# The down projection of 18 f tiles by Strassen's recursion, in three rounds

## The chip, the core and the metric

The kernel runs on one NeuronCore of a Trainium2 chip. The metric is the device time of one execution in microseconds (us); lower is better. The engines are TensorE (PE, matmuls), VectorE (DVE), ScalarE (ACT), GpSimd (POOL, hardly used here) and SyncE (SP, which issues the transfers).

## The reference

One layer of a diffusion backbone on 128 context and 512 latent tokens, 640 in all, with 1024 channels: modulation from a condition vector, an mLSTM and a convolution branch with an output projection, and then the gated MLP, to which the change belongs:

```python
h2 = rmsnorm(x, p['norm2_g']) * (1 + sc2) + sh2
gate, val = jnp.split(jnp.einsum('btd,df->btf', h2, p['w_up']), 2, axis=-1)
gate = dwconv_grid(gate, p['ffn_dw_w'], p['ffn_dw_b'])      # 3x3; on context width 3
x = x + g2 * jnp.einsum('btf,fd->btd', jax.nn.gelu(gate) * val, p['w_down'])
...
return final rmsnorm(x)
```

All is float32. `w_down` is 2816 x 1024: 22 tiles of 128 rows (the f tiles) by 8 tiles of 128 output channels (m). `g2` is one of six vectors that a 1024 x 6144 matrix makes from the condition.

## The kernel before

Activations lie channels first: a tile holds 128 channels and the 640 tokens, in two halves of 320 (`HALF`). A float32 product is made of three faster ones: each operand is split into a high part, rounded to the type fp32r, and a low part, the rest (hi and lo), and `three` adds hi x hi, hi x lo and lo x hi in one PSUM accumulator. ACT makes the high part by a copy, DVE the low part by a subtraction. Weights come in groups of eight 128 x 128 blocks (`BLOCKS`, in the order of use; `load` fetches a group to one of `NST` = 3 buffers `wst`, `prep` makes `wh` and `wl`, `NWT` = 3 of each).

The program's order is fixed when it is built: each engine runs its own list of instructions strictly in that order and waits by semaphores. `_Order` sets it: it follows the emission of the matmuls with an estimate of time and puts in between what the other engines have to do. A side task is a generator (`spawn`), which `step` carries on after every third of a product; `later` puts small pieces of DVE work into lanes, which are filled in where DVE has room, and `need(tag)` emits all that is left of a tag at once. In lane 20 stand the products of the condition with the rest of its matrix (`ada_tile`, in the trace `junk<-ad`, 128 of them, DVE alone); the last 32 carry the tag `g2`, the gate of the MLP's residual.

The MLP goes by f tiles. `ffn_tile(f)` emits the 48 matmuls of the gate half and the 48 of the value half (8 channel tiles, three products, two halves). ACT copies the gate to a grid buffer (`gbuf`), nine taps of the convolution run on DVE (`ffn_tap`, into `acc`), ACT applies gelu (`ge`), DVE multiplies with the value in PSUM, and ACT and DVE split the result (`ah`, `al`; the last tiles in another pool as `acth`, `actl`). Two lists set the stages: `UPS` (f 0 to 11, then 12 to 21) and `DNS` (f 0 to 10 after the first, f 11 to 21 after the second up stage). The first down stage makes each of the eight output tiles from 11 f tiles with 66 matmuls of 128 x 128 x 320, and `residual` adds it to `x2[m]` with three DVE operations (`x<-mm,mods,x`: context and latent tokens have different gates, so the first half is two pieces). Ahead of it `need("g2")` stands in the up stage, before tile 8. The second down stage runs by token parts, first 384 tokens (`dnA`; three output tiles begin without the last f tile), then 256 (`dnB`), each followed by the final norm (`final`) and the output's transfers.

PSUM has three pairs of accumulators (`mm`) and two single ones (`ps`).

Of the kernel before, what the change touches and what calls it, by code (L numbers as in the profile page):

```python
# [9 lines left out]
F32 = mybir.dt.float32  # L10
F32R = mybir.dt.float32r
# [4 lines left out]
P = 128  # L16
# [41 lines left out]
HOLE = 600.0  # L60
NB = 15
# [9 lines left out]
NST = 3  # L71
# [10 lines left out]
def _blocks():  # L82

    b = []
    held = {0: 2, 1: 3}
    for k in range(KD):
        b += [(nm, k, m) for nm, m in FIRST]
    for nm, m in ORDER:
        if nm == "v":
            held[len(b) // GB] = len(b) // GB + NWT  # L90
            held[len(b) // GB + 1] = 0
            b += [("v", k, 2 * m + i) for k in range(KD) for i in range(2)]
        else:
# [30 lines left out]

class _Timed:
# [192 lines left out]
def tile_trunk(  # L318
# [79 lines left out]
    ready = {}  # L398
    lines = {}

    def load(g):
        if g in stage or g in ready or g >= NGRP:
            return
        t = od.ring("st", sp.tile([P, GB * P], F32, tag="st", name="wst"), NST)
        Q.dma_start(t, w_d[g])
        stage[g] = t

    def prep(g):

# [12 lines left out]

        ready[g] = (hi, lo)
        lines[g] = od.spawn(parts())

    state = {"g": -1}

    def W(b, width=P):
        g, o = divmod(bidx[b], GB)
        if g > state["g"]:  # L430
            state["g"] = g
            held = HELD.get(g)
            for gg in range(g, g + NWT if held is None else held):
                prep(gg)
            if g >= NSTART:
                for gg in range(g + NWT, g + NWT + NST - 1):
                    load(gg)
# [716 lines left out]
    def A2(shape, dt=F32, name="b"):  # L1154
        return ap2.tile(shape, dt, tag="B", name=name)
# [181 lines left out]
    def ffn_gate(f, pgt):  # L1337
        od.need(("ffn", f - 2))
        g = gb_[f % 2]
        S.activation(g[:, 0:NCTX], pgt[:, 0, 0:NCTX], AF.Copy)  # L1340
        S.activation(lat_rows(g)[:, 0:3, 0:GRID_W], pgt[:, 0, NCTX:TH].rearrange("p (r w) -> p r w", w=GRID_W), AF.Copy)
        S.activation(lat_rows(g)[:, 3:8, 0:GRID_W], pgt[:, 1, 0:TH].rearrange("p (r w) -> p r w", w=GRID_W), AF.Copy)
        accs[f] = acc = A([P, TF], name="acc")
        for i in range(9):
            od.later(("ffn", f), lambda i=i: ffn_tap(f, g, acc, i), f % 2)

    def ffn_out(f, pvt):
        while od.waits(("ffn", f)):
# [9 lines left out]
        if f in range(0, NACT2) or f in range(NFH + 1, NFH + 1 + NACT2):  # L1358
            hi, lo = A2([P, T], F32R, "ah"), A2([P, T], F32R, "al")
        else:  # L1360
            hi, lo = A([P, T], F32R, "acth"), A([P, T], F32R, "actl")
        yield
        S.activation(hi, ge, AF.Copy)
        yield
        V.tensor_sub(lo, ge, hi.bitcast(F32))
        acts[f] = (hi, lo)

    def ffn_act(f, pvt):
        t_act[f] = od.spawn(ffn_out(f, pvt))
# [32 lines left out]
        mhalf(mat, 1, range(KD), h2, rng, pt=pts[2][:, h, 0:TH])  # L1402
    ffn_gate(1, pts[2])
    ffn_act(1, mtile("up", NF + 1, range(KD), h2))
    for f in UPS[0][2:]:
        if f == NACT2 - 2:
            od.need("g2")
        ffn_tile(f)
    ks = DNS[0]
    od.finish(t_act[UPS[0][-1]])  # L1410
    for m in range(8):
        pt = dn(mtile, "dn", m, ks)
        for h in range(2):
            residual(x2[m], pt[:, h, 0:TH], g2c[:, m, :], HALF[h])
    for f in ks:
        acts.pop(f)
    for f in UPS[1]:
        ffn_tile(f)


    ks = DNS[1]

    PARTS = [slice(0, TL), slice(TL, T)]

    def final(h, sums, adds):
# [13 lines left out]
        for j in range(0, KD, 2):  # L1439
# [19 lines left out]
    od.finish(t_f)  # L1459
    pools["stack"].close()  # L1460
# [1 line left out]
def _columns(v):  # L1462
# [129 lines left out]
```

## Time and profile before

| | |
|---|---|
| median of 3 runs | 976.29 us (974.4 to 976.96) |
| profiled execution | 975.71 us, span 973.5 us |
| PE | busy 946.8 us (97%), 6700 matmuls |
| DVE | busy 735.1 us (76%), 1348 instructions |
| ACT | busy 362.2 us (37%), 658 instructions |
| mean granted PE clock | 0.993 of full speed |

PE's busy time counts overlapping matmuls, so what one costs is read from the distance between starts. Lines are L139 for every instruction of the engines, since the wrapper `_Timed` issues them all; groups are told apart by the names of their tiles. From 540 us on the trace shows the MLP: up tiles to 665 us, the first down stage to 745 us, up tiles to 888 us, `dnA` to 930 us, `dnB` to 962 us, the last norm and output to 973.5 us.

### The profile page before, as it was taken

The numbers are of one execution on the slowest core, as the hardware profiler recorded it, in microseconds if no ns is written. First come the engines' busy times: TensorE is split into PE (matmuls) and PEld (weight loads), VectorE is DVE, ScalarE is ACT, GpSimd is POOL, SyncE is SP. The second block draws the span as 40 slices with busy tenths as digits, with TensorE's granted clock in tenths as the row PEclk, the third lists the DMA queues.
The fourth block names the chain that finished last, engine by engine and source line by source line (L and its number), as shares of the span: only waits on it lengthen the run. The fifth ranks groups of instructions, "written<-read, shape, count | busy, mean of one in ns | idle before, by whom it ended". The sixth has DMA issues, their size and how long they took to land.

```text
span 973.5 us, 16460 instructions
## 1 busy us (share of the span) xinstructions
PE 946.8 (97%) x6700; PEld 924.2 (95%) x6700; DVE 735.1 (76%) x1348; ACT 362.2 (37%) x658; POOL 6.0 (1%) x41
## 2 busy tenths in 40 slices
PE   5999999999999999999999999899999999999996
PEld 2899999999998999999989999899999999999995
DVE  3849989998897988898879778985323777675565
ACT  5553434245634422224674323232111232323342
POOL 0100000000000000000000000000000000000000
PEclk9999999999999999999999999999999999999998
DMA  9635122211242365567443221522222222123353
GB/s 355 245 104 87 45 76 66 74 47 45 87 141 71 104 196 189 201 233 251 147 135 102 77 79 63 163 87 65 82 71 65 88 68 84 65 88 94 123 170 113
DMA packets 38971, 113.01 MB, mean 116 GB/s; under 512 B 4336, under 2 KB 7280, under 8 KB 38896
## 3 DMA queue, kind: packets, MB, share of 16 engines
q1 hardware_dynamic: 38896, 111.96, 35.7%
q8 instruction: 53, 0.87, 0.4%
q14 instruction: 22, 0.18, 0.1%
HBM read 108.79 MB, written 3.15 MB: 115 GB/s over the span
## 4 chain that ended last, share of the span: by engine, by line
PE 92%; DVE 4%; ACT 2%; issue 1%; DMA 1%; SPq 0%; DVEq 0%; ACTq 0%
PE mm L139 84%; PE ps L139 8%; DVE junk L139 1%; DVE acc L139 1%; DMA x<-in_xT 1%; DVE wl L139 0%; ACT wh L139 0%; ACT h L139 0%; ACT L139 0%; DVE rsy L139 0%; DVE yo L139 0%; ACT h2h L139 0%; DVE rst L139 0%; ACT sq L139 0%; SPq L139 0%
## 5 line engine op out<-in xcount | busy, mean ns | idle before, releaser
L139 ACT ACTIVATE wh<-wst 128x1024 fp32r<-128x1024 f32 x145 | 152.9, 1057 | 197.1 <-PE mm L139 166.8
L139 DVE TENSOR_TENSOR wl<-wst,wh 128x1024 fp32r<-128x1024 f32 x145 | 176.5, 1220 | 56.2 <-ACT wh L139 55.9
L139 PE MATMUL mm<-h2h,wl 128*128 128x320 f32 x704 | 164.9, 310 | 2.4 <-DVE wl L139 2.4
L139 PE MATMUL mm<-h2h,wh 128*128 128x320 f32 x704 | 165.0, 310 | 0.6 <-ACT h2h L139 0.6
L139 PE MATMUL mm<-h2l,wh 128*128 128x320 f32 x704 | 164.8, 310 | 0.4 <-DVE h2l L139 0.4
L139 PE MATMUL mm<-hh,wh 128*128 128x320 f32 (+2 forms) x576 | 134.3, 312 | 3.5 <-ACT wh L139 2.5
L139 PE MATMUL mm<-hl,wh 128*128 128x320 f32 (+2 forms) x576 | 133.7, 311 | 0.0
L139 PE MATMUL mm<-hh,wl 128*128 128x320 f32 (+2 forms) x576 | 133.4, 310 | 0.0
L139 DVE SCALAR_TENSOR_TENSOR acc<-gbuf,cols,acc 128x455 f32<-128x455 f32 (+2 forms) x176 | 129.7, 742 | 4.4
L139 PEld LDWEIGHTS mm<-h2h,wl 128*128 128x128 f32 x704 | 119.2, 189 | 2.8 <-DVE wl L139 2.7
L139 PEld LDWEIGHTS mm<-h2h,wh 128*128 128x128 f32 x704 | 119.3, 189 | 1.3 <-ACT h2h L139 1.2
L139 PEld LDWEIGHTS mm<-h2l,wh 128*128 128x128 f32 x704 | 119.1, 188 | 1.1 <-DVE h2l L139 1.0
L139 DVE SCALAR_TENSOR_TENSOR z<-glu,cols,z 128x641 f32<-128x641 f32 (+14 forms) x120 | 102.2, 889 | 0.8
L139 PEld LDWEIGHTS mm<-hh,wh 128*128 128x128 f32 x576 | 96.0, 188 | 5.8 <-ACT wh L139 3.0
L139 PEld LDWEIGHTS mm<-hl,wh 128*128 128x128 f32 x576 | 96.6, 188 | 2.2 <-issue 1.3
L139 PEld LDWEIGHTS mm<-hh,wl 128*128 128x128 f32 x576 | 96.9, 189 | 0.7 <-issue 0.7
L139 PE MATMUL mm<-ah,wl 128*128 128x320 f32 (+2 forms) x320 | 85.6, 308 | 0.0
L139 PE MATMUL mm<-ah,wh 128*128 128x320 f32 (+2 forms) x320 | 85.4, 307 | 0.0
L139 PE MATMUL mm<-al,wh 128*128 128x320 f32 (+2 forms) x320 | 85.4, 307 | 0.0
L139 DVE SCALAR_TENSOR_TENSOR junk<-ad,cb 128x512 bf16<-128x512 f32 x128 | 81.8, 686 | 0.1
L139 PEld LDWEIGHTS mm<-ah,wl 128*128 128x128 f32 x320 | 56.8, 188 | 0.1
L139 PEld LDWEIGHTS mm<-al,wh 128*128 128x128 f32 x320 | 56.8, 188 | 0.0
(224 smaller groups left out, 1284.2 us busy)
## 6 DMA issues: line engine op xcount, KB each, us to landing
wst<-in_w SPq DMA_DIRECT2D x145, 512.0 KB, 3.6
ad<-in_ada SPq DMA_DIRECT2D x64, 256.0 KB, 3.0
adst<-in_ada SPq DMA_DIRECT2D x16, 512.0 KB, 10.2
x<-in_xT SPq DMA_DIRECT2D x16, 320.0 KB, 5.7
out_yT<-x SPq DMA_DIRECT2D x8, 192.0 KB, 4.3
cb<-in_crow SPq DMA_DIRECT2D x4, 256.0 KB, 5.0
out_yT<-yo SPq DMA_DIRECT2D x4, 256.0 KB, 2.5
Ca<-in_cst SPq DMA_DIRECT2D x1, 516.0 KB, 6.8
```

The source lines that it names most:

```text
L139: return fn(*args, **kw)
```

## The change

For f 0 to 17 the down projection is done in three rounds of six f tiles (`ROUNDS`), each after the up tiles it needs and one more (`UPS` has four lists now). A round takes three pairs of f tiles and, one after another, four groups: q = 0 to 3 is the pair of output tiles m1 = 2q and m2 = 2q + 1. With an f pair, an output pair and the two token halves, the product is one of 2 x 2 blocks, and Strassen's recursion (in Winograd's form) needs seven block products for eight. A block product here is nine matmuls of 320 columns (three f pairs, three parts), a group 63 matmuls instead of 72. The f tiles 18 to 21 stay with `dnA` and `dnB` (`LASTF`).

The seven weight forms of a group (`FORMS`; three 128 x 128 blocks side by side, 384 columns) are made on the core from two loaded groups: four sums on DVE (`sf`), and for each form a high part on ACT and a low part on DVE, both now in one buffer, a `wh` or a `wl` in turn (`prep_form`); `ahead` keeps six forms prepared. Of each f pair the activations get seven forms of 320 columns (`x_form`: four differences `tf` and `tg`, seven high and seven low parts `xf`). The intermediate sums stay in PSUM: three accumulators, `pa` with four of the products one after another, `pb` with two, `pd` with one, and `residual` reads an accumulator after each product, ten DVE operations a group. `need("g2")` moves to the start of round 0. The centre tap of the convolution goes from DVE to ACT, and at the end `final` of both parts is waited for.

```diff
-UPS = [list(range(0, NFH + 1)), list(range(NFH + 1, NF))]
-DNS = [list(range(0, NFH)), list(range(NFH, NF))]
+ROUNDS = [list(range(6 * r, 6 * r + 6)) for r in range(3)]
+LASTF = list(range(18, NF))
+UPS = [list(range(0, 7)), list(range(7, 13)), list(range(13, 19)), list(range(19, NF))]
+NPR = 3
+FORMS = ["A11", "S1", "S2", "A12", "S3", "S4", "A22"]
+READS = [("S1", "S3", "A22"), ("A11", "S2", "A12", "S3", "S4")]
+FW_ = NPR * P
...
+    def prep_form(g, j):
...
+                src = sums_[g, nm] = A([P, FW_], name="sf")
+                if nm == "S1":
+                    V.tensor_add(src, a21, a22)
+                else:
+                    x, y = {"S2": (sums_.get((g, "S1")), a11), "S3": (a11, a21), "S4": (a12, sums_.get((g, "S2")))}[nm]
+                    V.tensor_sub(src, x, y)
...
+            S.activation(hi, src, AF.Copy)
+            yield
+            V.tensor_sub(lo, src, hi.bitcast(F32))
...
-        if dh == 0 and dw == 0:
-            V.tensor_scalar(acc[:, 0:GF], g[:, 0:GF], col("ffn_w", 9 * f + 4), col("ffn_b", f),
-                            op0=ALU.mult, op1=ALU.add)
-            return
...
-        for i in range(9):
+        S.activation(acc[:, 0:GF], g[:, 0:GF], AF.Identity, scale=col("ffn_w", 9 * f + 4), bias=col("ffn_b", f))
+        for i in range(1, 9):
...
+    def pair_forms(f, ge):
+        p = f // 2
+        b1, b2 = ge[:, HALF[0]], ge[:, HALF[1]]
+        if f % 2 == 0:
+            t = A([P, 2, TH], name="tf")
+            V.tensor_sub(t[:, 0, :], b2, b1)
+            ges[p] = (ge, t)
+            yield from x_form(p, "B11", b1)
+            yield from x_form(p, "T1", t[:, 0, :])
+            return
...
+        for nm, src in (("T2", t[:, 1, :]), ("B21", b1), ("T3", u[:, 0, :]), ("B22", b2), ("T4", u[:, 1, :])):
+            yield from x_form(p, nm, src)
...
-    for f in UPS[0][2:]:
-        if f == NACT2 - 2:
+    def dn_round(r):
+
+        fs = ROUNDS[r]
+        for f in fs:
+            od.finish(t_act[f])
+        if r == 0:
             od.need("g2")
...
+            for pt, wn, xn, opens, outs in (
+                    (pa, "A11", "B11", True, [(m1, 0)]),
+                    (pb, "S1", "T1", True, [(m2, 1)]),
+                    (pa, "S2", "T2", False, [(m1, 1)]),
+                    (pd, "A12", "B21", True, [(m1, 0)]),
+                    (pa, "S3", "T3", False, [(m2, 1)]),
+                    (pb, "S4", "B22", False, [(m1, 1)]),
+                    (pa, "A22", "T4", False, [(m2, 0)])):
+                hi, lo = form(g, FORMS.index(wn))
+                for i in range(NPR):
+                    o = slice(i * P, (i + 1) * P)
+                    three([(pt, slice(0, TH))], (hi[:, o], lo[:, o]), xf[fs[2 * i] // 2, xn],
+                          opens and i == 0, i == NPR - 1, again=not opens)
+                form_at.pop(("f", g, FORMS.index(wn)))
+                for m, h in outs:
+                    residual(x2[m], pt, g2c[:, m, :], HALF[h])
...
+    for i, fs in enumerate(UPS):
+        for f in fs[2:] if i == 0 else fs:
+            ffn_tile(f)
+        if i < len(ROUNDS):
+            dn_round(i)
+    ks = LASTF
...
-        t_f = od.spawn(final(h, sums, adds))
-    od.finish(t_f)
+        t_f.append(od.spawn(final(h, sums, adds)))
+    od.finish(*t_f)
```

How the lists of instructions read at three places (an entry ends in the columns of its output; xN is a run of N; L139 is before, L161 after). First DVE around the remaining conditioning products. Before, in the up stage, between the taps of one tile and the weights and the value product of the next:

```order
L139 SCALAR_TENSOR_TENSOR acc<-gbuf_5545,cols,acc 128x455 x5
L139 SCALAR_TENSOR_TENSOR acc<-gbuf_5545,cols,acc 128x454
L139 SCALAR_TENSOR_TENSOR junk,modp<-ad,cb 128x512 x21
L139 TENSOR_TENSOR mods<-modp 128x16
L139 TENSOR_TENSOR mods<-mods,cols 128x16
L139 TENSOR_TENSOR wl<-wst,wh 128x1024
L139 TENSOR_TENSOR ge<-ge,mm 128x640
L139 TENSOR_TENSOR wl<-wst,wh 128x1024 x2
```

After, between the taps of f 6 and the first residual of round 0 (two weight sums ahead of it):

```order
L161 SCALAR_TENSOR_TENSOR acc<-gbuf_5543,cols,acc 128x455 x4
L161 SCALAR_TENSOR_TENSOR acc<-gbuf_5543,cols,acc 128x454
L161 SCALAR_TENSOR_TENSOR junk,modp<-ad,cb 128x512 x22
L161 TENSOR_TENSOR mods<-modp 128x16
L161 TENSOR_TENSOR mods<-mods,cols 128x16
L161 TENSOR_TENSOR sf<-wst 128x384
L161 TENSOR_TENSOR sf<-wst,sf 128x384
L161 SCALAR_TENSOR_TENSOR x_4836<-mm,mods,x_4836 128x128
L161 SCALAR_TENSOR_TENSOR x_4836<-mm,mods,x_4836 128x192
```

The burst stood before weights and stands before a residual now, with one product more. Second, DVE in a down stage. Before, one output tile of the first down stage (three residual pieces and one or two weight groups):

```order
L139 SCALAR_TENSOR_TENSOR x_4840<-mm,mods,x_4840 128x128
L139 SCALAR_TENSOR_TENSOR x_4840<-mm,mods,x_4840 128x192
L139 SCALAR_TENSOR_TENSOR x_4840<-mm,mods,x_4840 128x320
L139 TENSOR_TENSOR wl<-wst,wh 128x1024 x2
L139 SCALAR_TENSOR_TENSOR x_4842<-mm,mods,x_4842 128x128
```

After, in round 0 from group q = 2 to q = 3, from the residual of its fifth product (S3) to the first one of the next group:

```order
L161 SCALAR_TENSOR_TENSOR x_4846<-mm,mods,x_4846 128x320
L161 TENSOR_TENSOR sf<-wst 128x384
L161 TENSOR_TENSOR sf<-sf,wst 128x384
L161 SCALAR_TENSOR_TENSOR x_4844<-mm,mods,x_4844 128x320
L161 TENSOR_TENSOR sf<-wst 128x384
L161 TENSOR_TENSOR wl<-wst,wl 128x384
L161 TENSOR_TENSOR wh<-wst,wh 128x384
L161 TENSOR_TENSOR wh<-sf,wh 128x384
L161 SCALAR_TENSOR_TENSOR x_4846<-mm,mods,x_4846 128x128
L161 SCALAR_TENSOR_TENSOR x_4846<-mm,mods,x_4846 128x192
L161 TENSOR_TENSOR sf<-wst,sf 128x384
L161 TENSOR_TENSOR wl<-sf,wl 128x384 x2
```

Between two residuals stand up to four small weight operations, and the next entry is the first residual of the new group. Third, PE in group q = 2 (`mm_6902` holds `pa` and `pb`, `mm_6903` is `pd`): the products S1 and S2 and the start of A12, with what their first matmuls wait for. Before, such a stretch reads:

```order
L139 MATMUL mm_7273<-ah_5930,wh_7132 128x320 [waits DVE_49,PE_49]
L139 MATMUL mm_7273<-ah_5930,wh_7132 128x320
L139 MATMUL mm_7273<-al_5931,wh_7132 128x320 x2
L139 MATMUL mm_7273<-ah_5930,wl_7133 128x320 x2
L139 MATMUL mm_7273<-ah_5946,wh_7132 128x320 x2
L139 MATMUL mm_7273<-al_5947,wh_7132 128x320 x2
L139 MATMUL mm_7273<-ah_5946,wl_7133 128x320 x2
```

After:

```order
L161 MATMUL mm_6902<-xf_5949,wl_6841 128x320 [waits DVE_49,Activation_49]
L161 MATMUL mm_6902<-xf_5949,wl_6841 128x320 x2
L161 MATMUL mm_6902<-xf_6097,wl_6841 128x320 x3
L161 MATMUL mm_6902<-xf_6424,wl_6841 128x320 x3
L161 MATMUL mm_6902<-xf_5965,wh_6855 128x320 [waits DVE_49,Activation_49]
L161 MATMUL mm_6902<-xf_5965,wh_6855 128x320 x2
L161 MATMUL mm_6902<-xf_6229,wh_6855 128x320 x3
L161 MATMUL mm_6902<-xf_6526,wh_6855 128x320 x3
L161 MATMUL mm_6903<-xf_5985,wl_6866 128x320 [waits PE_49]
```

An accumulator waited for DVE once per output tile; now a product every nine matmuls does, and S2 writes where A11's residual has read. At the end of the program DVE's last entries were the eight products of the last 256 tokens (`yo`); three products of the first 384 tokens (`x_4846`, `x_4848`, `x_4850`) follow them now.

More of the change, by code (lines that the diff above doesn't have):

```diff
@@ L107, in _blocks @@
     b += [("up", k, NF + 1) for k in range(KD)]
-    for i, (fs, ks) in enumerate(zip(UPS, DNS)):
+    pairs = {}
+    for i, fs in enumerate(UPS):
         for f in fs[2:] if i == 0 else fs:
@@ L399, in tile_trunk, with load @@
     lines = {}
-    def load(g):
-        if g in stage or g in ready or g >= NGRP:
+    live = {}
+    raws = {}
+    def load(g, must=True):
+        if g in stage or g in ready or g in raws or g >= NGRP:
             return
+        while len(live) >= NST:
+            if not must:
+                return
+            od.force(next(t for t in lines.values() if not t[2]))
         t = od.ring("st", sp.tile([P, GB * P], F32, tag="st", name="wst"), NST)
-        Q.dma_start(t, w_d[g])
+        n = 2 * FW_ if g in PAIRS or g - 1 in PAIRS else GB * P
+        Q.dma_start(t[:, 0:n], w_d[g, :, 0:n])
         stage[g] = t
+        live[g] = 1 if n == GB * P else len(READS[g not in PAIRS])
     def prep(g):
@@ L421, in parts @@
             V.tensor_sub(lo, src, hi.bitcast(F32))
+            live.pop(g)
         ready[g] = (hi, lo)
         lines[g] = od.spawn(parts())
+    sums_, form_at = {}, {}
+    def prep_form(g, j):
+        u = ("f", g, j)
+        if u in form_at:
+            return
+        for gg in (g, g + 1):
+            if gg not in raws:
+                load(gg)
+                raws[gg] = stage.pop(gg)
+        t2, t1 = raws[g], raws[g + 1]
+        a21, a22, a11, a12 = t2[:, 0:FW_], t2[:, FW_:2 * FW_], t1[:, 0:FW_], t1[:, FW_:2 * FW_]
+        tag = ("wh", "wl")[UNIT_AT[u] % 2]
+        w = od.ring(tag, wp.tile([P, GB * P], F32R, tag=tag, name=tag), NWT)
+        hi, lo = w[:, 0:FW_], w[:, 512:512 + FW_]
+        nm = FORMS[j]
+        def parts():
+            yield from od.until(t1, t2)
+            if nm[0] == "A":
+                src = {"A11": a11, "A12": a12, "A22": a22}[nm]
+            else:
+                while nm in ("S2", "S4") and (g, {"S2": "S1", "S4": "S2"}[nm]) not in sums_:
+                    yield
+                src = sums_[g, nm] = A([P, FW_], name="sf")
+                if nm == "S1":
+                    V.tensor_add(src, a21, a22)
+                else:
+                    x, y = {"S2": (sums_.get((g, "S1")), a11), "S3": (a11, a21), "S4": (a12, sums_.get((g, "S2")))}[nm]
+                    V.tensor_sub(src, x, y)
+                if nm in ("S2", "S4"):
+                    sums_.pop((g, {"S2": "S1", "S4": "S2"}[nm]))
+                if nm in ("S3", "S4"):
+                    sums_.pop((g, nm))
+                yield
+            S.activation(hi, src, AF.Copy)
+            yield
+            V.tensor_sub(lo, src, hi.bitcast(F32))
+            for gg in (g, g + 1):
+                if nm in READS[gg - g]:
+                    live[gg] -= 1
+                    if not live[gg]:
+                        live.pop(gg)
+        if nm == "A22":
+            raws.pop(g), raws.pop(g + 1)
+        form_at[u] = (hi, lo)
+        lines[u] = od.spawn(parts())
@@ new lines, in ahead @@
+    def ahead(i):
+        room = 2 * NWT
+        while i < len(UNITS):
+            kind, g, j = UNITS[i]
+            room -= 2 if kind == "c" else 1
+            if room < 0:
+                break
+            if kind == "c":
+                prep(g)
+            else:
+                prep_form(g, j)
+            i += 1
+        n = 0
+        while i < len(UNITS) and n < NST - 1:
+            kind, g, j = UNITS[i]
+            for gg in (g,) if kind == "c" else (g, g + 1):
+                if n < NST - 1 and gg not in raws:
+                    load(gg, False)
+                    n += 1
+            i += 1 if kind == "c" else len(FORMS) - j
@@ L426, in tile_trunk, with form @@
+    def form(g, j):
+        u = ("f", g, j)
+        ahead(UNIT_AT[u])
+        od.force(lines.pop(u))
+        return form_at[u]
     state = {"g": -1}
@@ L432, in W @@
             held = HELD.get(g)
[L433 to L437, printed above, removed]
+            if g < NSTART or held is not None:
+                for gg in range(g, g + NWT if held is None else held):
+                    prep(gg)
+                if g >= NSTART:
+                    for gg in range(g + NWT, g + NWT + NST - 1):
+                        load(gg)
+            else:
+                ahead(UNIT_AT["c", g, 0])
         if g in lines:
@@ L441, in W, with three @@
         return hi[:, o * P:o * P + width], lo[:, o * P:o * P + width]
-    def three(out, whl, xhl, first, last, shared=0):
+    def three(out, whl, xhl, first, last, shared=0, again=False):
         (wh, wl), (xh, xl) = whl, xhl
         for i, (o, s) in enumerate(out):
-            PE.matmul(o, lhsT=wh, rhs=xh[:, s], start=first and (i, shared) != (0, 2), stop=False)
+            PE.matmul(o, lhsT=wh, rhs=xh[:, s], start=first and (i, shared) != (0, 2), stop=False,
+                      skip_group_check=again)
         od.step()
         for o, s in out:
-            PE.matmul(o, lhsT=wh, rhs=xl[:, s], start=False, stop=False)
+            PE.matmul(o, lhsT=wh, rhs=xl[:, s], start=False, stop=False, skip_group_check=again)
         od.step()
         for i, (o, s) in enumerate(out):
-            PE.matmul(o, lhsT=wl, rhs=xh[:, s], start=False, stop=last and (i, shared) != (0, 1))
+            PE.matmul(o, lhsT=wl, rhs=xh[:, s], start=False, stop=last and (i, shared) != (0, 1),
+                      skip_group_check=again)
         od.step()
```

89 lines of the change are left out of this document (64 added, 25 removed).

## The prediction

> **What bounds the kernel now.** I read the page first (busy shares, the chain), then the waits of PE, then the clock and the timelines of PE and DVE from 540 us on, where the MLP runs; all that the change touches lies there.
>
> ```profile
> span 973.5 us, 16460 instructions
> PE 946.8 (97%) x6700; PEld 924.2 (95%) x6700; DVE 735.1 (76%) x1348; ACT 362.2 (37%) x658; POOL 6.0 (1%) x41
> PE 92%; DVE 4%; ACT 2%; issue 1%; DMA 1%; SPq 0%; DVEq 0%; ACTq 0%
> ...
> PE mm L139 <- DVE wl L139: 2.4, 1, 2.4
> ...
> 700.12 0.46 PE L139 MATMUL mm<-ah,wh 128*128 128x320 f32 x2
> ...
> 702.76 0.46 PE L139 MATMUL mm<-ah,wh 128*128 128x320 f32 x2
> ...
> 899.95 0.34 PE L139 MATMUL mm<-ah,wl 128*128 128x384 f32 x1
> ...
> 900.99 0.34 PE L139 MATMUL mm<-ah,wl 128*128 128x384 f32 x1
> ...
> 940.06 0.28 PE L139 MATMUL mm<-ah,wl 128*128 128x256 f32 x1
> ...
> 941.76 0.28 PE L139 MATMUL mm<-ah,wl 128*128 128x256 f32 x1
> ```
>
> PE is the bound: it carries 92% of the chain and, from 550 us to its last product, waits once, 2.4 us. So a matmul taken away is time gained, as long as PE still waits for nobody. The price of one is its spacing, not its duration (they overlap): 18 of 320 columns in 2.64 us are 0.1467 each, 6 of 384 in 1.04 us are 0.1733, 15 of 256 in 1.70 us are 0.1133.
>
> The one wait stands where DVE works off the rest of the conditioning products (`junk<-ad`), 21 in a row; the next weights queue behind them:
>
> ```profile
> 607.86 0.68 DVE L139 SCALAR_TENSOR_TENSOR junk<-ad,cb 128x512 bf16<-128x512 f32 x1
> ...
> 620.27 0.69 DVE L139 SCALAR_TENSOR_TENSOR junk<-ad,cb 128x512 bf16<-128x512 f32 x1
> ...
> 622.58 0.82 PE L139 MATMUL mm<-h2h,wl 128*128 128x320 f32 x2 [2.44 <-DVE wl L139]
> ...
> 623.00:626.00 3.00, 3.00 (x13) 3.00 (x12) 3.00 (x4) 0.74 (x1) 0.00 (x0) 0.50 0.67 188
> ...
> 331.62 0.53 PE L139 MATMUL mm<-zh,wh 128*128 128x320 f32 x2 [1.01 <-DVE ga L139]
> ...
> 332.00:333.00 1.00, 1.00 (x9) 1.00 (x8) 1.00 (x4) 0.00 (x0) 0.00 (x0) 1.00 0.23 90
> ```
>
> Twenty starts in 12.41 us make 0.62 us each. The burst costs PE only 2.44 us because PE holds prepared weights for the rest of it. After the wait the granted clock is 0.50 for some 3.2 us, which loses half of that; a wait of 1.01 us left the clock at 1.00.
>
> **The matmuls.** Before, the down projection has 528 matmuls of 320 columns, 264 of 384 and 264 of 256: 77.5 + 45.8 + 29.9 = 153.2 us. After, the three rounds have 12 groups of 63 (756 of 320), the last four f tiles 96 of 384 and 96 of 256: 110.9 + 16.6 + 10.9 = 138.4 us. That is 14.8 us less. The wait of 622.58 also leaves its old place: 2.44 us and 1.6 us of clock, 4.0 us less.
>
> **What DVE is asked to do.** These rows price its steps:
>
> ```profile
> 623.17 2.35 DVE L139 TENSOR_TENSOR wl<-wst,wh 128x1024 fp32r<-128x1024 f32 x2
> ...
> L139 DVE TENSOR_TENSOR wl<-wst,wh 128x1024 fp32r<-128x1024 f32 x65 | 79.3, 1221 | 42.6 <-ACT wh L139 42.4
> L139 DVE TENSOR_TENSOR sq<-sq,sq 128x384 f32<-128x384 f32 x6 | 3.3, 557 | 1.8 <-ACT sq L139 1.8
> L139 DVE TENSOR_TENSOR h2l<-h,h2h 128x320 fp32r<-128x320 f32 x16 | 7.8, 486 | 1.8 <-ACT h2h L139 1.7
> L139 DVE SCALAR_TENSOR_TENSOR x<-mm,mods,x 128x128 f32<-128x128 f32 x16 | 5.6, 348 | 30.3 <-PE mm L139 30.3
> L139 DVE SCALAR_TENSOR_TENSOR x<-mm,mods,x 128x192 f32<-128x192 f32 x8 | 3.3, 408 | 0.0
> L139 DVE SCALAR_TENSOR_TENSOR x<-mm,mods,x 128x320 f32<-128x320 f32 x8 | 4.3, 542 | 0.0
> L139 DVE SCALAR_TENSOR_TENSOR acc<-gbuf,cols,acc 128x455 f32<-128x455 f32 x90 | 62.4, 694 | 2.9
> L139 DVE TENSOR_SCALAR acc<-gbuf,cols 128x649 f32<-128x649 f32 x17 | 10.5, 619 | 36.2 <-ACT gbuf L139 36.2
> L139 ACT ACTIVATE h<-h,mods,a 128x320 f32<-128x320 f32 x8 | 5.1, 640 | 0.0
> L139 ACT ACTIVATE h<-h,mods,a 128x128 f32<-128x128 f32 x8 | 3.8, 478 | 0.0
> L139 DVE TENSOR_TENSOR ge<-ge,mm 128x640 f32<-128x640 f32 x18 | 14.8, 821 | 9.4 <-ACT ge L139 9.1
> ```
>
> Two subtractions of 1221 take 2.35 us together, so work that waits for nothing follows 0.09 us faster than its duration: 0.47 for 384 columns (the nearest row is of the same size and engine), 0.40 for 320, and 0.60 for a residual pair of 128 and 192, 0.46 for one of 320. A group has seven low parts and four sums of 384, three residual pairs and four of 320: 5.2 + 3.6 = 8.8 us, where PE needs 63 x 0.1467 = 9.24. On average it fits, barely. It does not fit in place: the first product of a group and the third share one accumulator, so the third waits until the residual of the first has read it, and that residual stands in DVE's queue behind next group's weight forms.
>
> *From a group's fifth product (S3) to the next group's third (S2).* PE has four products in between, 4 x 1.32 = 5.28 us, less an estimated 0.2 until a product can be read. DVE has in this order: residual 0.46; two sums, the second on the first, 1.03; residual 0.46; a sum and three low parts 1.9; a pair 0.60; a sum and two low parts 1.4; a pair 0.68 to its end: 6.5 us. PE waits 1.4 us, with wake-ups 1.5. Nine such group changes (three a round): 13.5 us. Below, 0 if DVE's order leaves no overrun; above, 2.5 each. The last tile of each up stage (f 6, 12, 18) also leaves work inside the rounds: `ge` 0.74, differences and low parts of 0.4, up to three taps of 0.61, in all about 9 us; I put half on PE's path, the other half into the slots where DVE waits for a product: 5 us. The sum of the rounds is 18.5 us, with ends 0 and 30.
>
> **The opening of round 0.** The 22 products left of the conditioning now stand between the taps of f 6 and the first residual. How late the taps end is read from the last tile of before:
>
> ```profile
> 877.04 0.83 ACT L139 ACTIVATE gbuf<-mm 128x128 f32<-128x128 f32 x3 [2.04 <-PE mm L139]
> ...
> 886.09 0.69 DVE L139 SCALAR_TENSOR_TENSOR acc<-gbuf,cols,acc 128x454 f32<-128x454 f32 x1
> ```
>
> That is 9.7 us after the gate's matmuls end. In the new order two subtractions of 1024 are gone from the stretch (-2.3), two of 384 and five of 320 are in it (+2.9), and the centre tap runs on ACT with its per-channel scale (0.62 becomes about 0.92, an estimate: 640 ns for 320 columns and, from the rows of 320 and 128, 0.84 ns for each further one): 10.6 us. The value half of f 6 takes PE 48 x 0.1467 = 7.0 us of that. So the burst starts 3.6 us into the round and takes 22 x 0.62 = 13.6; two small sums, two sums of 384 and the first residual pair add 1.9: 19.1 us. PE reaches the third product after 2.64 us and waits 16.5 us, where nothing covers it any more. Then comes half clock, 1.6 us. If DVE were a whole tile's slack earlier it could still not start before the gate of f 6, so the ends are 14 and 18 us.
>
> **The end.**
>
> ```profile
> 890.37 0.82 DVE L139 TENSOR_TENSOR al<-ge,ah 128x640 fp32r<-128x640 f32 x1
> ...
> 930.18 0.74 DVE L139 SCALAR_TENSOR_TENSOR x<-mm,mods,x 128x128 f32<-128x128 f32 x2 [1.97 <-PE mm L139]
> ...
> 934.12 0.26 DVE L139 TENSOR_SCALAR rsv<-ps 128x96 f32<-128x96 f32 x1 [3.19 <-ACT rsy L139]
> ...
> L139 DVE SCALAR_TENSOR_TENSOR x<-x,cols,ps 128x384 f32<-128x384 f32 x8 | 4.9, 608 | 0.0
> ```
>
> The final norm of the first 384 tokens (3.2 us of waiting for the square root, then eight products of 0.53) ran under 30 us of matmuls; now they are 10.9. DVE's work there (residuals, squares, two weight subtractions, the norm) no longer fits; three of the eight products land behind the last tile's output (+1.6), and a wait of PE or DVE of about 1.4 before: 3 us, ends 1.6 and 6. At the entry to the last part, f 21 is ready 14.2 us after its gate (877.04 to 891.19, the end of `al`), and its queues are as before. The cover was the value half, 7.0 us, and 90 matmuls of 384, 15.6; now it is 7.0 and 27 of them, 4.7: PE waits 2.5 us, ends 0 and 4.
>
> **The sum.** 975.7 us (this execution: span 973.5 and 2.2 around it; the median of the runs is 0.6 higher) - 14.8 - 4.0 + 16.5 + 1.6 + 18.5 + 2.5 + 3.0 = 999.0. Costed at nothing: 12 us more of ACT (37% busy), the forms of the activations in the up stages (96 matmuls, 14.1 us, a tile, of which DVE idles 4.2 by the row below, and they add 1 to 2), and the weight transfers, whose bytes hardly change; if that cover went, the next up stage would be late by the same microsecond or two per tile.
>
> ```profile
> 800.00:850.00 50.00, 50.00 (x343) 50.00 (x342) 35.16 (x45) 16.31 (x32) 0.00 (x0) 1.00 0.23 74
> ```
>
> **A rule on the clock.** The row: 2.44 us of waiting brought 0.50, 1.01 us did not. The Trainium skill (TensorE: Matmul & The Clock Gate, HAM oscillation — how this bites in real kernels) asks for no idle gaps above about 3.4 us. By that rule the nine waits of 1.5 us leave the clock alone and the sum stays; but the same rule would have spared the wait at 622.58, which the trace does not, so the measurement decides and a fall at each of them stays a rival.
>
> **Rivals.**
> - *The work fits.* If DVE reached each residual before PE needs its accumulator, the opening of round 0 included, only the matmuls count: 975.7 - 14.8 - 4.0 + 2.5 + 3.0 = 962. It decides at the overrun: an operation of 384 columns would have to start every 0.31 us instead of 0.47, and the burst would have to lie elsewhere. For it speaks the average (8.8 against 9.24). Chance 0.09.
> - *Only the opening waits.* The group changes are hidden after all: 962.4 + 18.1 = 980.5. It hangs on the order of eleven small operations, which I price from rows of other places. Chance 0.16.
> - *The clock falls at the group changes too.* Nine times 1.6 us: 999 + 14 = 1013. Waits of 1.5 to 2.4 us lie between the two rows. Chance 0.12.
>
> **How the numbers follow.** My forecast has 0.63 and by itself reaches from 987 to 1008. About 0.3% (3 us) is what a measurement here can tell from no change. Somewhat over a third of "only the opening waits" may come out within that of before (0.06), the rest is slower: 0.10 + 0.63 + 0.12 = 0.85; faster 0.09. The range 984 to 1012 leaves out the fast rival, about half of the opening-only one, and the far side of the clock rival.
>
> **What would show it.** A wait of PE on DVE of about 16 us at the start of round 0 with DVE full of `junk`, then clock 0.50; nine gaps of 1 to 3 us before third products, put down to DVE `x`; DVE over 90% busy in the rounds; 756 matmuls that read `xf`, spaced 0.1467; three `x` of 384 columns after the last `yo`. I am wrong if PE runs through the rounds without gaps, or if the gap of 16 us is missing because the burst ended before f 6.

## The result, and the profile after

The changed kernel takes 1047.31 us (median of 4 runs, 1046.84 to 1050.04) against 976.39 us before: a ratio of 1.0736, 95% interval 1.0712 to 1.076. The forecast of slower was right, its size was not: 71 us more than before instead of 23, and 35 us above the upper end of the range. The profiled execution took 1047.01 us.

The page after: the span, the busy times, and the chain of work that ended last (shares of the span by engine).

```profile
span 1044.8 us, 16760 instructions
PE 951.2 (91%) x6592; PEld 917.4 (88%) x6592; DVE 817.0 (78%) x1610; ACT 409.6 (39%) x784; POOL 6.0 (1%) x41
PE 79%; DVE 13%; ACT 4%; issue 2%; DMA 1%; SPq 0%; DVEq 0%; ACTq 0%
```

PE's share of the chain went from 92% to 79%, DVE's from 4% to 13%. The waits of PE (us in total, how many, the longest) say on what:

```profile
PE mm L161 <- DVE x L161: 56.9, 43, 17.4
```

Before, no wait of this kind was in the list; now 43 products wait for a residual. One of them is the opening of round 0: the burst stands where it was predicted, but the wait begins one product early, at the second product (S1) and not at the third. Timeline of the changed kernel (start, duration, instruction; in brackets how long the engine had been idle, and who released it):

```profile
592.87 0.69 DVE L161 SCALAR_TENSOR_TENSOR junk<-ad,cb 128x512 bf16<-128x512 f32 x1
...
605.73 0.69 DVE L161 SCALAR_TENSOR_TENSOR junk<-ad,cb 128x512 bf16<-128x512 f32 x1
...
607.70 0.67 DVE L161 SCALAR_TENSOR_TENSOR x<-mm,mods,x 128x128 f32<-128x128 f32 x2
...
608.52 2.74 PE L161 MATMUL mm<-xf,wl 128*128 128x320 f32 x9 [17.44 <-DVE x L161]
```

The 22 conditioning products run from 592.87 to 606.4 without a gap, the first residual follows, and PE has waited 17.44 us at S1. Nine matmuls then take 2.74 us instead of 1.48: half clock.

The surprise is inside the groups. The same timeline, one whole group of round 0 with its residuals (rows of weights and other DVE work left out). Which product is which follows from the residuals: `128x128 ... x2` is one of the first token half, `128x320` one of the second.

```profile
641.16 1.56 PE L161 MATMUL mm<-xf,wl 128*128 128x320 f32 x9 [1.63 <-DVE x L161]
642.76 0.55 DVE L161 SCALAR_TENSOR_TENSOR x<-mm,mods,x 128x320 f32<-128x320 f32 x1 [1.28 <-PE mm L161]
...
643.46 1.55 PE L161 MATMUL mm<-xf,wh 128*128 128x320 f32 x9 [0.74 <-ACT wl L161]
644.86 1.48 PE L161 MATMUL mm<-xf,wl 128*128 128x320 f32 x9
645.05 0.55 DVE L161 SCALAR_TENSOR_TENSOR x<-mm,mods,x 128x320 f32<-128x320 f32 x1 [1.28 <-PE mm L161]
646.18 1.47 PE L161 MATMUL mm<-xf,wh 128*128 128x320 f32 x9
647.69 0.55 DVE L161 SCALAR_TENSOR_TENSOR x<-mm,mods,x 128x320 f32<-128x320 f32 x1 [0.64 <-PE mm L161]
648.39 1.56 PE L161 MATMUL mm<-xf,wl 128*128 128x320 f32 x9 [0.74 <-DVE x L161]
649.99 0.55 DVE L161 SCALAR_TENSOR_TENSOR x<-mm,mods,x 128x320 f32<-128x320 f32 x1 [0.69 <-PE mm L161]
650.60 1.59 PE L161 MATMUL mm<-xf,wh 128*128 128x320 f32 x9 [0.64 <-DVE x L161]
652.02 1.48 PE L161 MATMUL mm<-xf,wl 128*128 128x320 f32 x9
654.32 0.67 DVE L161 SCALAR_TENSOR_TENSOR x<-mm,mods,x 128x128 f32<-128x128 f32 x2
655.14 1.56 PE L161 MATMUL mm<-xf,wh 128*128 128x320 f32 x9 [1.63 <-DVE x L161]
```

In order of the starts these are S1 (641.16), S2, A12, S3, S4 (648.39), A22 (650.60), the next group's A11 and its S1. Four of seven wait: S1, S2, S4 and A22. Each starts right after the residual of the product just before it, whatever that product's accumulator was. (The profile puts the wait at 643.46 down to ACT, whose `wl` ended there as well; the residual from 642.76 to 643.31 ended at nearly the same moment.) And ahead of three of these residuals (642.76, 647.69, 649.99) DVE itself had been idle for 1.28, 0.64 and 0.69 us: it was not late, it was waiting for PE. A group takes 13.98 us, S1 to S1, where its 63 matmuls need 9.24.

The rounds as stretches (start and end, length; busy time and instructions of PE, weight loads, DVE, ACT, POOL; granted clock as a share of full speed; the last two on transfers), rounds 0, 1, 2 and the group above:

```profile
589.60:666.00 76.40, 44.62 (x255) 40.63 (x254) 53.57 (x132) 16.53 (x31) 0.00 (x0) 0.84 0.25 78
750.37:809.47 59.10, 43.82 (x254) 39.60 (x253) 40.13 (x88) 16.84 (x31) 0.00 (x0) 0.94 0.23 69
893.87:951.47 57.60, 42.60 (x254) 38.52 (x253) 39.72 (x86) 16.65 (x30) 0.00 (x0) 0.97 0.23 71
641.16:655.14 13.98, 10.22 (x64) 9.27 (x64) 9.29 (x22) 3.55 (x7) 0.00 (x0) 1.00 0.21 69
```

Together 193.1 us, where 756 matmuls at 0.1467 need 110.9: 82.2 us too many. DVE is busy 68 to 70% there, not over 90%.

### The profile page after: what moved, and what is told of

The parts are those of the page before. It is cut to its first block, busy times and chain, and to the rows that moved or that the text cites. A ratio compares the mean times of both kernels' runs of the same rounds, so it can differ in the third digit from the quotient of the medians.

```text
span 1044.8 us, 16760 instructions
## 1 busy us (share of the span) xinstructions
PE 951.2 (91%) x6592; PEld 917.4 (88%) x6592; DVE 817.0 (78%) x1610; ACT 409.6 (39%) x784; POOL 6.0 (1%) x41
## 4 chain that ended last, share of the span: by engine, by line
PE 79%; DVE 13%; ACT 4%; issue 2%; DMA 1%; SPq 0%; DVEq 0%; ACTq 0%
PE mm L161 72%; PE ps L161 7%; DVE x L161 3%; DVE wl L161 2%; DVE acc L161 2%; DVE junk L161 1%; DVE sf L161 1%; DMA wst<-in_w 1%; DVE wh L161 1%; ACT wh L161 1%; DVE xf L161 1%; DMA x<-in_xT 1%; ACT L161 0%; DVE rsy L161 0%; ACT h L161 0%
## 5 line engine op out<-in xcount | busy, mean ns | idle before, releaser
L161 ACT ACTIVATE wh<-wst 128x1024 fp32r<-128x1024 f32 (+1 forms) x138 | 135.4, 982 | 133.6 <-PE mm L161 109.3
L161 DVE SCALAR_TENSOR_TENSOR acc<-gbuf,cols,acc 128x455 f32<-128x455 f32 (+2 forms) x176 | 129.9, 742 | 58.0 <-ACT acc L161 55.5
L161 PE MATMUL mm<-h2h,wh 128*128 128x320 f32 x704 | 164.5, 309 | 0.6 <-ACT h2h L161 0.6
L161 PE MATMUL mm<-h2l,wh 128*128 128x320 f32 x704 | 164.3, 309 | 0.4 <-DVE h2l L161 0.4
L161 PE MATMUL mm<-h2h,wl 128*128 128x320 f32 x704 | 164.1, 309 | 0.0
L161 DVE TENSOR_TENSOR wl<-wst,wh 128x1024 fp32r<-128x1024 f32 x120 | 145.8, 1221 | 18.2 <-ACT wh L161 18.1
L161 PE MATMUL mm<-hh,wh 128*128 128x320 f32 (+2 forms) x576 | 134.3, 312 | 3.5 <-ACT wh L161 2.5
L161 PE MATMUL mm<-hl,wh 128*128 128x320 f32 (+2 forms) x576 | 133.5, 311 | 0.0
L161 PE MATMUL mm<-hh,wl 128*128 128x320 f32 (+2 forms) x576 | 133.5, 310 | 0.0
L161 PEld LDWEIGHTS mm<-h2h,wh 128*128 128x128 f32 x704 | 118.8, 188 | 1.3 <-ACT h2h L161 1.2
L161 PEld LDWEIGHTS mm<-h2l,wh 128*128 128x128 f32 x704 | 118.7, 188 | 1.1 <-DVE h2l L161 1.0
L161 PEld LDWEIGHTS mm<-h2h,wl 128*128 128x128 f32 x704 | 118.6, 188 | 0.1
L161 DVE SCALAR_TENSOR_TENSOR x<-mm,mods,x 128x320 f32<-128x320 f32 (+3 forms) x144 | 60.3, 446 | 64.0 <-PE mm L161 63.8
L161 PE MATMUL mm<-xf,wl 128*128 128x320 f32 x378 | 68.8, 329 | 40.3 <-DVE x L161 38.1
L161 DVE SCALAR_TENSOR_TENSOR z<-glu,cols,z 128x641 f32<-128x641 f32 (+14 forms) x120 | 102.3, 890 | 0.8
L161 PEld LDWEIGHTS mm<-xf,wl 128*128 128x128 f32 x378 | 60.6, 201 | 46.5 <-ACT wh L161 20.6
L161 PEld LDWEIGHTS mm<-hh,wh 128*128 128x128 f32 x576 | 96.0, 188 | 5.8 <-ACT wh L161 3.0
L161 PEld LDWEIGHTS mm<-hl,wh 128*128 128x128 f32 x576 | 96.5, 188 | 1.8 <-issue 1.3
L161 PEld LDWEIGHTS mm<-hh,wl 128*128 128x128 f32 x576 | 96.8, 188 | 0.7 <-issue 0.7
L161 PE MATMUL mm<-xf,wh 128*128 128x320 f32 x378 | 67.9, 326 | 21.8 <-DVE x L161 18.1
L161 PEld LDWEIGHTS mm<-xf,wh 128*128 128x128 f32 x378 | 59.7, 198 | 27.8 <-ACT wh L161 8.3
L161 DVE SCALAR_TENSOR_TENSOR junk<-ad,cb 128x512 bf16<-128x512 f32 x128 | 81.7, 687 | 0.0
```

The lines of the kernel that those rows point to most:

```text
L161: return fn(*args, **kw)
```

## Experiments

Ratios are to the kernel before, timed beside each run (medians 973.75 to 977.11 us). A result without a ratio is one run.

**Two accumulators in one tile (e1, e2, e3).** The code makes `pa` and `pb` as the two halves of one PSUM tile `ab`. Theory A: a product that writes one half waits until DVE has read the other. Theory B: DVE is late because of its own queue.

e1 puts `pb` into a single accumulator that lies free in the rounds:

```diff
-            pa, pb, pd = ab[:, 0, 0:TH], ab[:, 1, 0:TH], shared[:, q % 2, 0:TH]
+            pa, pb, pd = ab[:, 0, 0:TH], ps()[:, 0:TH], shared[:, q % 2, 0:TH]
```

> Each group's second accumulator (S1, S4) gets a PSUM tile of its own instead of the other half of the tile that the first accumulator lies in. Theory A (two accumulators in one tile: a product waits until DVE has read the other half): the waits of S1, S2, S4 and A22 of 1.63, 0.74, 0.74 and 0.64 us shrink to some 0.3 us for S2 alone, a group takes about 10.0 us instead of 13.98, and the time is 995 to 1006 us. Rival B (DVE is late with the residuals because of its other work): nothing changes, 1044 to 1050 us.

Measured: 1004.13 us, ratio to before 1.0301 (1.0274 to 1.0327), so 43.2 us less by one line. In the program the first matmul of S1 no longer has a wait on DVE (`-` the changed kernel, `+` e1), and S2 waits for A11's residual, as the prediction had it, where it waited for that of S1:

```
-L161 MATMUL mm<-xf,wl 128x320 [waits DVE_49,Activation_49]
+L161 MATMUL ps<-xf,wl 128x320 [waits Activation_49]
```

Its timeline, the products S2 of two groups:

```profile
635.36 1.56 PE L161 MATMUL mm<-xf,wh 128*128 128x320 f32 x9 [1.00 <-DVE x L161]
...
646.26 1.56 PE L161 MATMUL mm<-xf,wl 128*128 128x320 f32 x9 [0.99 <-DVE x L161]
```

And its stretches, rounds 0, 1, 2, then the group between those two products:

```profile
591.17:652.95 61.78, 41.37 (x255) 39.38 (x254) 52.85 (x132) 16.66 (x31) 0.00 (x0) 0.86 0.31 96
737.33:781.36 44.03, 38.52 (x254) 36.99 (x253) 39.22 (x88) 16.76 (x31) 0.00 (x0) 1.00 0.29 93
865.75:910.78 45.03, 39.85 (x255) 38.51 (x254) 38.80 (x86) 16.33 (x30) 0.00 (x0) 0.96 0.29 91
635.36:646.26 10.90, 9.74 (x64) 9.24 (x64) 9.10 (x22) 4.46 (x8) 0.00 (x0) 1.00 0.27 81
```

The only wait over 0.2 us left in that group is S2's at the group change, and the three rounds are 42.3 us shorter, 14.6, 15.1 and 12.6 each. Theory A holds: the four waits go, and the time is in its range. Only S2's wait is longer than expected, 1.0 us against 0.3, and so is the group, 10.90 us against 10.0.

e2 gives `pb` its own place and puts A12's accumulator `pd` into the other half of `pa`'s tile, so that theory A moves the waits:

```diff
-            pa, pb, pd = ab[:, 0, 0:TH], ab[:, 1, 0:TH], shared[:, q % 2, 0:TH]
+            pa, pb, pd = ab[:, 0, 0:TH], ps()[:, 0:TH], ab[:, 1, 0:TH]
```

> The second accumulator gets a tile of its own, and the third (A12's) now lies in the other half of the first one's tile. Theory A: the waits move with the tile: S1, S4 and A22 run on, and A12 and S3, which ran without a wait, wait 0.7 us each; a group takes about 11.4 us, the time is 1011 to 1021 us. Rival B: as e1 says, 1044 to 1050 us. Rival C (a product can never start while DVE reads any PSUM tile that the product before it wrote): every product waits, about 1060 us.

Measured: 1038.16 us. Timeline of a part of one group:

```profile
640.18 1.56 PE L161 MATMUL mm<-xf,wh 128*128 128x320 f32 x9 [0.99 <-DVE x L161]
641.78 0.55 DVE L161 SCALAR_TENSOR_TENSOR x<-mm,mods,x 128x320 f32<-128x320 f32 x1 [0.35 <-PE mm L161]
642.39 2.71 PE L161 MATMUL mm<-xf,wl 128*128 128x320 f32 x9 [0.65 <-DVE x L161]
645.13 0.68 DVE L161 SCALAR_TENSOR_TENSOR x<-mm,mods,x 128x128 f32<-128x128 f32 x2 [2.80 <-PE mm L161]
645.96 2.74 PE L161 MATMUL mm<-xf,wh 128*128 128x320 f32 x9 [0.86 <-DVE x L161]
648.50 1.85 PE L161 MATMUL ps<-xf,wl 128*128 128x320 f32 x9
```

Stretches for the clock: two in that part (0.56 and 0.50), and one around the same three waits at the next group change (0.99, 0.64 and 0.86 us, from 655 to 660 us), where it stays at 1.00:

```profile
642.00:646.00 4.00, 2.75 (x10) 2.38 (x10) 1.01 (x3) 0.58 (x2) 0.00 (x0) 0.56 0.28 102
646.00:649.00 3.00, 3.00 (x11) 3.00 (x12) 0.26 (x1) 0.00 (x0) 0.00 (x0) 0.50 0.00 0
655.00:662.00 7.00, 4.97 (x30) 4.51 (x31) 4.36 (x10) 1.73 (x2) 0.00 (x0) 1.00 0.70 222
```

The waits moved as theory A says: A12 (642.39, 0.65 us) and S3 (645.96, 0.86 us), which had run on in the changed kernel, now wait; S4 (648.50), A22 and S1 run on. Theories B and C would not move them. The time was 17 us above theory A's range: S2 still waits 0.99 us, and the clock fell in rounds 0 and 2 (granted 0.79 and 0.88 over the round; round 1 kept 1.00). How the 17 us divide between the two was not measured.

e3 leaves out the sums of the weights, four DVE operations of each group:

```diff
-                if nm == "S1":
-                    V.tensor_add(src, a21, a22)
...
+                src = {"S1": a21, "S2": a11, "S3": a21, "S4": a12}[nm]
```

> Leaves out the sums of the weight tiles on DVE (S1 to S4 are split from single raw tiles), so DVE has four instructions, 2.2 us, less in each of the 12 groups; accumulators as in the changed kernel. Theory A: only the wait of S1, where DVE is behind, shrinks, from 1.63 to about 1.0 us; the other waits keep their 0.64 to 0.74 us; 1036 to 1044 us. Rival B: the group shrinks by DVE's 2.2 us, 1018 to 1025 us.

Measured: 1051.25 us, no gain at all and outside both ranges. A later group of round 0 (S4, A22, then S1 and S2 of the next) still waits four times, 0.94, 0.74, 0.86 and 0.74 us, 3.3 us in place of 3.75. S1's wait shrinks, as theory A has it, but S4's grows. From S1 to S1 such a group takes 13.46 us, 0.5 less than 13.98, where DVE has 2.2 us less to do: theory B is out. The time was lost elsewhere: one wait of 3.27 us in round 0 has half clock behind it. Why that wait is so long was not followed up.

**The opening (e4, e6, e10).** e4 puts `od.need("g2")` ahead of up tile 4:

> DVE's 22 products of the gate of the second residual are put ahead of up tile 4 instead of ahead of round 0's first residual. Theory (the third product of round 0 waits for nothing else): the wait of 17.4 us at 608.5 falls under 5 us and the low clock after it goes; up tiles wait for DVE 2 to 5 us; 1028 to 1037 us. Rival (DVE has no room, and the wait only moves into the up tiles): 1043 to 1050 us.

Measured: 1040.8 us. Its two waits on DVE in that region:

```profile
569.07 0.90 PE L161 MATMUL mm<-h2h,wl 128*128 128x320 f32 x2 [6.85 <-DVE wl L161]
...
604.27 2.77 PE L161 MATMUL mm<-xf,wl 128*128 128x320 f32 x9 [4.19 <-DVE x L161]
```

6.85 + 4.19 = 11.04 us in place of 17.44, 6.4 us less, and the time fell by 6.5 us, to between the two ranges: some of the wait only moved. The cause is the one predicted, but DVE has little room for it elsewhere. e6, with more on POOL as well, and e10, without POOL, both on top of e1, spread the gate's products over five up tiles (`some` takes a number of them off the lane; cut to the place of the call):

```diff
         for f in fs[2:] if i == 0 else fs:
+            if i == 0:
+                od.some("g2", 5)
             ffn_tile(f)
```

> As e5, and also the four sums of each activation pair go to POOL, and DVE's products of the second residual's gate are put ahead of up tiles 2 to 6, five at each. Theory: the wait of 16 us at the start of round 0 falls under 5 us and the half clock after it goes, some 14 us below e5: 974 to 984 us. Rival (DVE is full in the up tiles, so they wait instead): 985 to 992 us.

> As e1, with the gate's products on DVE put ahead of up tiles 2 to 6, five at each; no work on POOL. It tells why e6 still waited 13.9 us at the start of round 0. Theory (POOL's sums slowed DVE: its taps took up to 1.24 us each there against 0.68 us): without POOL the wait is 4 to 7 us and the time 989 to 996 us. Rival (DVE is too full in the up tiles with or without POOL): the wait stays over 11 us, 998 to 1004 us.

Measured: e6 997.7 us, ratio 1.0237 (1.0213 to 1.026), and e10 998.39 us, 1.0238 (1.0219 to 1.0257); e6 is above both ranges, e10 in the rival's. The opening wait was 13.94 us in e6 and 8.67 us in e10. Timelines of DVE and POOL, e6 first, then the same subtraction in e10:

```profile
599.12 1.38 POOL L161 TENSOR_TENSOR sf<-wst 128x384 f32<-128x384 f32 x1
...
599.58 1.28 DVE L161 TENSOR_TENSOR xf<-tf,xf 128x320 fp32r<-128x320 f32 x1
```

```profile
598.19 0.48 DVE L161 TENSOR_TENSOR xf<-tf,xf 128x320 fp32r<-128x320 f32 x1
...
605.39 2.74 PE L161 MATMUL mm<-xf,wh 128*128 128x320 f32 x9 [8.67 <-DVE x L161]
```

While POOL adds, DVE's subtraction takes 1.28 us instead of 0.48; of the 18 with these names none takes over 0.49 us in e10. So POOL made the wait worse, as the theory says (e5 and e11 below, where only the sums of the weights move, show it too), and without POOL it is still 8.67 us, because DVE is full (39.75 of 40 us busy from 560 to 600 us in e10), as the rival says. The truth lies between the two.

**What is left in the rounds (e5, e11).** e5 is e1 with the sums of the weights on POOL (`G.tensor_add` and `G.tensor_sub` for `V.`), e11 is e10 with the same:

> As e1 (second accumulator in a tile of its own), and the sums of the weight tiles go from DVE to POOL. In e1 one wait of 1.0 us per group is left, at S2, whose accumulator DVE releases late behind weight work at the group change. Theory (DVE's order at the group change, 2.2 us of sums per group): that wait goes, 1.24 us with its refill for nine or more groups, 990 to 996 us. Rival (the handback itself is too long for one product between): the wait stays and the time is that of e1, 1001 to 1007 us. Second rival: POOL is slow and the weights come late, over 1010 us.

> As e10, with the sums of the weight tiles on POOL (as in e5); the sums of the activations stay on DVE. It asks whether the two gains add up. Theory (the sums of the weights shorten rounds 1 and 2 from 44 to 41.3 us each, and the opening keeps e10's wait of 8.7 us): 990 to 994 us. Rival (POOL slows DVE in round 0 as in e5 and e6, where the opening grew by 3 to 5 us, and eats the gain): 996 to 1001 us.

Measured: e5 997.7 us, e11 990.64 us (ratio 1.0135, 1.0117 to 1.0153). The stretches of e11, rounds 0 to 2:

```profile
592.19:645.23 53.04, 39.38 (x254) 38.72 (x253) 45.48 (x91) 19.47 (x37) 15.02 (x13) 0.87 0.25 78
729.63:771.15 41.52, 38.26 (x254) 36.98 (x253) 37.10 (x74) 17.20 (x31) 14.70 (x11) 1.00 0.28 89
855.54:897.32 41.78, 38.18 (x255) 37.03 (x254) 36.21 (x72) 17.11 (x30) 14.23 (x11) 1.00 0.30 89
```

The waits of S2 at the three group changes of round 0, 0.99 to 1.31 us in e1, are gone in both. Rounds 1 and 2 come to 41.5 and 41.8 us (41.42 and 41.21 in e5, 44.0 and 45.0 in e1), but not all waits there are gone: of 5.5 and 5.2 us in e1, 3.3 and 3.6 us are left in e11. But beside POOL the opening grew, to a wait of 19.57 us in e5 (16.12 in e1) and 13.22 in e11 (8.67 in e10), so e5 just missed its range and e11 is in it with the rival's opening.

**The rounds without Strassen (e7, e9).** e7 keeps the rounds and the rest of the change and multiplies plainly:

```diff
+        for m in range(8):
+            pt = mtile("dn", m, fs, [acts[f] for f in fs])
+            for h in range(2):
+                residual(x2[m], pt[:, h, 0:TH], g2c[:, m, :], HALF[h])
```

> The three rounds and the last part of four f tiles stay, the centre tap stays on ACT and the gate's 22 products stay ahead of round 0's first residual, but each round multiplies plainly: eight products for eight, two accumulators of a whole m tile in one PSUM tile, no sums. Theory (the loss is in Strassen's short products and their residuals): three free PSUM tiles cover 15.8 us of the opening, products of 5.3 us cover every handback, 974 to 984 us. Rival (the rounds, the entry and the end cost it whatever is multiplied): over 995 us.

Measured: 990.76 us, ratio 1.0158 (1.0136 to 1.0181), between the two. Its opening wait (timeline), and its three rounds as stretches:

```profile
608.45 0.87 PE L156 MATMUL mm<-ah,wh 128*128 128x320 f32 x2 [5.08 <-DVE ge L156]
```

```profile
592.64:642.39 49.75, 44.67 (x290) 44.43 (x289) 29.71 (x71) 7.93 (x10) 0.00 (x0) 0.93 0.32 101
726.78:769.02 42.24, 42.24 (x290) 42.24 (x289) 18.49 (x33) 7.93 (x10) 0.00 (x0) 1.00 0.26 83
853.42:895.66 42.24, 42.24 (x290) 42.24 (x289) 18.49 (x33) 7.93 (x10) 0.00 (x0) 1.00 0.24 83
```

Plain products of 5.28 us cover every residual: rounds 1 and 2 are 288 matmuls at 0.1467 and nothing else. Strassen's rounds would be 5.3 us shorter each if PE never waited; the best measured (e5) are 0.8 to 1.0 us shorter. And what e7 keeps of the change (the rounds, the opening, the entry and the end) costs 1.6%, some 15 to 17 us, although the centre tap on ACT, a gain by itself (e8 below), is in it. e9 takes one part of that away: the last three up tiles go ahead of round 2.

```diff
-UPS = [list(range(0, 7)), list(range(7, 13)), list(range(13, 19)), list(range(19, NF))]
+UPS = [list(range(0, 7)), list(range(7, 13)), list(range(13, NF)), []]
```

> As e7 (three rounds without Strassen), and the up tiles 19 to 21 go ahead of round 2 instead of behind it, so that the last part's four activations are ready when it starts. Theory (the entry to the last part costs 1.57, 1.07 and 0.93 us of waits and a half clock behind them): these go, 984 to 988 us. Rival (round 2 then waits, or the clock is not hit there): 989 to 992 us.

Measured: 984.47 us, as the theory has it, and the three waits at the entry are gone from its trace. In e7 the entry to the last part thus costs some 6 us: waits of 1.57, 1.07 and 0.93 us and the lower clock behind them.

**One part alone (e8).** The centre tap on ACT, put into the kernel before:

```diff
-        for i in range(9):
+        S.activation(acc[:, 0:GF], g[:, 0:GF], AF.Identity, scale=col("ffn_w", 9 * f + 4), bias=col("ffn_b", f))
+        for i in range(1, 9):
```

> The kernel before with one part of the change alone: the centre tap of the gate's convolution goes from DVE to ACT, once per f tile. Theory (the wait of 2.44 us at 622.58, with the half clock behind it, comes from DVE's backlog in the up tiles): DVE is some 0.4 us per tile further ahead there, the wait shrinks by 1 to 2.4 us, 971 to 974 us against 975.4. Rival (the backlog is the 22 products put ahead of up tile 8, whatever the taps cost): within 1 us of the kernel before.

Measured: 972.18 us against 975.12, ratio 0.9969 (0.9958 to 0.998): 0.3% less than the kernel before, a small gain, but each of its 7 runs is below each of the 11 beside it. DVE has room to put in more of the conditioning products earlier, so the burst is 16 of them instead of 21. The stretch in which the wait of 2.44 us stood has none:

```profile
600.00:640.00 40.00, 40.00 (x275) 40.00 (x275) 37.13 (x68) 14.49 (x26) 0.00 (x0) 1.00 0.34 112
```

## Why the prediction was right in direction and wrong in size

| term | predicted | measured |
|---|---|---|
| matmuls | -14.8 | -14.8 (spacing still 0.1467: 644.86 to 646.18 is nine) |
| wait at 622.58 and its clock | -4.0 | gone (e8, where only this wait goes: -2.9) |
| opening of round 0 | +16.5 | +17.4 (at S1; e1: 16.1 at S2) |
| rest of the rounds, clock included | +1.6 + 18.5 | +64.8 (82.2 less 17.4) |
| entry and end | +2.5 + 3.0 | +7.9 (what remains of 71.3 with -4.0 for the wait) |

The step that failed is "From a group's fifth product (S3) to the next group's third (S2)", the source of the 18.5. It let PE run the products in between, on the ground that a product waits only for its own accumulator. The order on each engine, and DVE's load (8.8 us a group, measured 9.1 to 9.3), were right; the dependence was not. Halves of one tile are one thing to the program's waits, so S1, S2, S4 and A22 each wait for the residual of the product before. That is 3.75 us of waits and some 1 us of refilling per group, twelve groups long, besides the clock. Over all three rounds the waits behind the opening are 44.6 us, 3.7 a group. The line `pa, pb, pd = ab[:, 0, ...], ab[:, 1, ...]` stood in the code, and S1's wait on DVE stood in the list of PE's instructions ahead of the prediction; the upper end of 30 did not allow for it.

The opening's size is partly luck, by the same step: its wait was priced from the third product and began at the second, 1.32 us sooner, while the first residual ended some 0.3 us earlier than forecast (607.70 + 0.67 is 18.8 us into the round, against 19.1). In e1, where S1 runs on, it is the predicted wait at the predicted place: 16.12 us before S2.

e1 removes just that, and the rest of the sum then nearly holds: 1004.1 us against the 999.0 forecast, with the predicted wait at the group change (1.4 forecast, 1.0 measured, at S2). So the direction was not luck: without the failed step the change is still slower. In e1 the rounds are 39.9 us over their matmuls, where the sum had 36.6, but they are made up otherwise: S2 waits at five of the nine group changes, 0.91 to 1.31 us, and in rounds 1 and 2 stand waits that the sum did not have, 2.08 us before the second group and 1.56 us for weights. That the totals are so close is partly luck.

Of the signs to look for, the 17 us wait amid `junk` and the half clock behind it came. So did the three `x` of 384 columns behind `yo`, 1.66 us at the end (1.6 forecast), and 756 matmuls that read `xf`, spaced 0.1467. The gaps before third products did not come as meant: in the group shown 3.0 of 3.75 us of waits are at other products, and the 0.74 us before S2 is for S1's residual. The one meant, for A11's, stands before S1, 1.63 us. DVE over 90% busy was wrong: a chain of product, residual, product leaves both engines partly idle, and no busy share shows it. The waits at the entry were 3.6 us against 2.5, and the sum had no clock behind them.

The rival on the clock was partly right. Waits and refilling apart, half clock came in all three rounds (granted 0.84, 0.94 and 0.97), though not at each group change. Of the 82.2 us, 62.0 are waits; the other 20.2 are refilling and clock, and how they divide was not measured by itself. "The work fits" fell with the opening; "only the opening waits" fell too, as even e1 waits at the group changes.

## What to carry to other kernels

Accumulators that are handed back separately belong in tiles of their own: before adding up what hides a handback, list for each product which tile, not which slice, its waits are about. When an algorithm saves matmuls by making the products shorter, price the cover it takes from what ran behind them: in rounds 1 and 2, products of 5.28 us hid every residual, while products of 1.32 us left waits even in tiles of their own (5.2 to 5.5 us a round in e1). And test the small parts alone: moving one tap to an engine with room gave the only gain over the kernel before.

## What the runs showed of the hardware that was not expected

- Waits under 2 us can halve the clock, and their lengths alone do not decide it. In e2, 0.99, 0.65 and 0.86 us within 6 us left it at 0.56 and 0.50 from 642 to 649 us; 0.99, 0.64 and 0.86 us at the next group change left it at 1.00. In the changed kernel, waits of 1.77 and 0.73 us open round 1, and the clock is 0.50 from 756.6 to 761 us; 1.77 and 0.74 us open round 2, and it is 1.00 from 897.1 to 904 us. What does decide it stays open. The Trainium skill (TensorE: Matmul & The Clock Gate, A second HAM failure mode: psum-queue depth-cycling) tells of small idles between groups of matmuls that make the clock swing; the trace agrees that it swings, not that each such row of idles does it. The rule weighed in the prediction, no gaps over about 3.4 us, would have let all of these pass.
- POOL slows DVE: 1.28 us against 0.48 for the same subtraction. The Trainium skill (SBUF — State Buffer, SBUF: two separate sides) says that a DVE operation with two inputs in SBUF and a POOL operation that reads SBUF lock each other out; the rows fit that.
- A handback with nothing between costs PE 0.64 to 0.74 us of idle, although the residual itself takes 0.55 us and DVE was free.
